# The up stage's results stored through POOL's DMA queue, and the third down operand loaded one stage earlier

## The chip, the cores and the metric

The kernel runs on one core of a Trainium2 chip. The metric is the device time of one execution in microseconds (us). Before the change three runs took 1323.78, 1328.26 and 1328.96 us, with a median of 1328.26 us.

## The reference

One transformer layer over 1024 latent tokens with 256 context tokens, in float32, with a model width of 1024. The part that matters here is its last one, the MLP, which is preceded by a modulated norm `h` of the mid-layer stream `x_mid`:

```python
def sq_relu_mlp(h, w1, w2):
    return jnp.square(jax.nn.relu(h @ w1)) @ w2

x = x_mid + gt_f * sq_relu_mlp(modulate(rms_norm(x_mid, g_ffn), sh_f, sc_f), w_ff1, w_ff2)
return rms_norm(x, g_final)
```

`w_ff1` is 1024 x 4096 and `w_ff2` is 4096 x 1024, so the activations between them are 1024 x 4096.

## The kernel before

**Arithmetic.** Every float32 operand of a product is split into a high and a low part (`split`, lines 102 to 104: a cast on ACT, line 103, then a subtraction on DVE, line 104). `mm3` (lines 96 to 100) then issues three matmuls: high by high (line 98), high by low (line 99), low by high (line 100).

**The up stage** (the first matrix of the MLP). Both MLP products are done with seven block products instead of eight (Strassen's scheme in Winograd's form). `w_ff1` is cut into 16 column groups p = 0 to 15 (`NP` is 16). For each p there are seven up products q = 1 to 7, and the list `order` (lines 1347 to 1352) says in which order the 112 pairs (p, q) are traced. The last eight are (15,2), (15,1), (14,3), (15,5), (15,6), (15,7), (15,4), (15,3). For each pair, `mm_1` issues 12 matmuls, and `post1` moves the result out of PSUM and combines it with the others. q = 6 and q = 7 add into the PSUM bank of q = 1, so the copies of lines 1177 and 1179 on ACT must have read the bank before the next of these products writes into it.

**The stores.** From one p come seven stores to DRAM: "a" after (p,1), 256 KB, and after (p,3) the blocks y, z and w, each as a high and a low part of 512 KB. `store_u` (lines 1146 to 1156) writes them. The high part is a cast on ACT into a new tile (line 1152), the low part a subtraction on DVE in place, and all seven DMAs are issued by SP (lines 1148, 1154, 1155). When they have landed, the tiles are free again.

**Tiles.** Nearly all large data lives in 45 equal tiles in SBUF (`Slots`, lines 35 to 50). A tile is taken from the front of a list of free ones when the code asks for it, and put at its end when the code is done with it. An instruction that writes into a reused tile waits until everything that used it before has finished, a store included. In the code's order the list holds 1 to 4 free tiles after the eight products from (0,7) to (3,6), behind which the first stores of y, z and w come, and 4 to 9 in the later regular part.

**The down stage** (the second matrix) goes through four blocks b of 1024 rows of `w_ff2`, with seven products each, `steps2 = (b, q)` with q in the order 2, 1, 6, 5, 3, 7, 4. One step is 48 matmuls. A step needs one operand from the stored activations (`load_u`: y, a, z, z, w, w, y) and one from `w_ff2` (B21, B11, B12 and B22 as loaded by `load_w2`, or their differences T1 to T3, made on DVE at line 1085 by `chain_w2`). `prep2` splits them. `load_u` issues the "a" blocks on SP's queue and y, z, w on POOL's (line 1237). `load_w2` issues on SP's (line 1211), as `load_w1` does for `w_ff1` (line 1092). The trace calls both weights `in_w_ff_dram`.

**The seam between the stages.** The loop over `order` already begins the down stage:

```python
        if s == len(order) - 11:
            load_w2(0, ("B21",))
            load_u(*steps2[0])
        if s == len(order) - 6:
            prep2(*steps2[0])
            load_w2(0, ("B11",))
            load_u(*steps2[1])
        if s == len(order) - 4:
            load_w2(0, ("B12", "B22"))
        if s == len(order) - 3:
            chain_w2(0)
        if s == len(order) - 2:
            prep2(*steps2[1])
```

The third step's operand, `steps2[2]` = (0,6), a z block, is loaded at the beginning of the first down step, and from then on each step s loads the operand of step s + 2 and prepares that of step s + 1. The tiles that `load_w2` gets for B12 and B22 of block 0 are those of z (low), w (high), w (low) and the working tile of p = 14. The tiles that `load_u` gets for the fourth step's operand (0,5) are those of y and z of p = 15, and `prep2` of (0,6) splits T2 into tiles of w of p = 15.

**Order on the engines.** The code's order is a priority. A planner sorts the instructions of every engine and queue by estimated times, so that an engine may hold a later line ahead of an earlier one. Each engine then works through its list in order and stops at the first instruction that has to wait.

Of the kernel before, what the change touches and what calls it, by code (L numbers as in the profile page):

```python
# [53 lines left out]
def hymba_block(ctx: ExitStack, tc: tile.TileContext, A, K, out):  # L54
    nc = tc.nc
    V, S, T, G = nc.vector, nc.scalar, nc.tensor, nc.gpsimd
# [7 lines left out]
    sl = Slots(slotp, NSLOT)  # L64
# [25 lines left out]
    def f(ap):  # L90
        return ap.bitcast(F32)

    def tt(o, a, b, op):
        V.tensor_tensor(out=o, in0=a, in1=b, op=op)  # L94
# [7 lines left out]
    def split(raw, hi, lo, eng=None):  # L102
        S.copy(out=hi, in_=raw)  # L103
        (eng or V).tensor_tensor(out=lo, in0=raw, in1=f(hi), op=ALU.subtract)  # L104
# [77 lines left out]
    order = "PDDPDDPPPPPPPPPP"  # L182
# [3 lines left out]
    for i, who in enumerate(order):  # L186
        q = (wa_pe if who == "P" else wa_dve)
        g, kt = q[sum(w == who for w in order[:i])]
        wa[g, kt] = load_wa(g, kt)
        if 3 <= i < 9:  # L190
            o, n, ap = rowsrc[i - 3]
# [194 lines left out]
    for t in range(NA):  # L386
# [8 lines left out]
        if t < NT:  # L395
            if t % 2 == 0:
                h = sl.get((2, 512))
# [139 lines left out]
    for i, t in enumerate(list(range(NT, NT + NC)) + list(range(NT))):  # L537
        if t % 2 == 0:
            h = sl.get((2, 512))
# [460 lines left out]
    for h in range(MH):  # L1000
        p = h // 2
# [40 lines left out]
    while pend:  # L1042
# [4 lines left out]
    NP, GB = FF // 256, 4  # L1047
    NB = NP // GB
    xm = [dramp.tile([P, 1024], F32, name=f"xm{t}") for t in range(NT)]
    ud = {(q, b, v): dramp.tile([P, n, GB, 512], F32, name=f"ud{q}{b}{v}")  # L1050
          for b in range(NB) for q, n in (("a", 1), ("y", 2), ("z", 2), ("w", 2))
          for v in ((0,) if q == "a" else (0, 1))}
# [30 lines left out]
    def pairop(eng, o, a, b, op):  # L1083
        for v in range(len(o)):
            eng.tensor_tensor(out=o[v][0], in0=a[v][0], in1=b[v][0], op=op)  # L1085
# [45 lines left out]
    def mm_1(p, q):  # L1131
        ps = bank(p, q)
        a = a1.pop((p, q))
        bh, bl = h2c[BOF[q]]
        for k in range(4):
            mm3(ps, a[0][:, 0, k], a[0][:, 1, k], bh[k // 2][0][:, k % 2, :], bl[k // 2][0][:, k % 2, :],
                q in (1, 2, 4, 5) and k == 0, k == 3, q in (3, 6, 7))
        sl.put(a)
        if p == NP - 1:
            sl.put(*bh, *bl)  # L1140
# [3 lines left out]
        S.activation(out=ap, in_=ap, func=AF.Square)  # L1144

    def store_u(q, p, r, ap):
        if q == "a":
            nc.sync.dma_start(out=ud[q, p // GB, 0][:, :, p % GB, :], in_=ap)
            return
        h = sl.get((2, 512), F32R)  # L1150
        lo = ap.bitcast(F32R)
        S.copy(out=h[0], in_=ap)  # L1152
        tt(lo, ap, f(h[0]), ALU.subtract)
        nc.sync.dma_start(out=ud[q, p // GB, 0][:, :, p % GB, :], in_=f(h[0]))
        nc.sync.dma_start(out=ud[q, p // GB, 1][:, :, p % GB, :], in_=f(lo))
        sl.put(h, r)

    def post1(p, q):
        ps = bank(p, q)
        if q == 2:  # L1160
            cq[p] = [sl.get((2, 512))]
            S.copy(out=cq[p][0][0][:, 0], in_=ps)
            unbank(p, q)
            return
        if q == 7:
            cq[p].append(sl.get((2, 512)))
        x_ = cq[p][0]
        c11, c12 = x_[0][:, 0], x_[0][:, 1]
        if len(cq[p]) > 1:
            y_ = cq[p][1]  # L1170
            c21, c22 = y_[0][:, 0], y_[0][:, 1]
        if q == 1:
            tt(c11, ps, c11, ALU.add)
            sqrelu(c11)
            store_u("a", p, x_, x_[0][:, 0:1])
        elif q == 6:
            S.copy(out=c12, in_=ps)
        elif q == 7:
            S.copy(out=c21, in_=ps)
            unbank(p, q)  # L1180
            tt(c22, bank(p, 5), c21, ALU.add)
        elif q == 4:
            tt(c21, c21, ps, ALU.subtract)
            unbank(p, q)
            sqrelu(c21)
            sqrelu(c22)
        elif q == 3:
            tt(c12, ps, c12, ALU.add)
            unbank(p, q)
            sqrelu(c12)  # L1190
            z, w = sl.get((2, 512)), sl.get((2, 512))
            s1, s2, s3, s4 = z[0][:, 0], z[0][:, 1], w[0][:, 0], w[0][:, 1]
            tt(s1, c12, c22, ALU.add)
            tt(s2, s1, c11, ALU.subtract)
            tt(s3, c11, c12, ALU.subtract)
            tt(s4, c21, s2, ALU.subtract)
            store_u("y", p, y_, y_[0])
            store_u("z", p, z, z[0])
            store_u("w", p, w, w[0])
            sl.put(x_)  # L1200
            cq.pop(p)
# [21 lines left out]
    def chain2_w2(b):  # L1223
        pairop(V, w2r[b, "B21"], w2r[b, "B21"], w2r[b, "T2"], ALU.subtract)
        w2r[b, "T4"] = w2r.pop((b, "B21"))
        sl.put(*w2r.pop((b, "T2")))
# [4 lines left out]
    def load_u(b, q):  # L1231
        n, k = UOF[q]
        vs = (0,) if n == "a" else (0, 1)
        ur[b, q] = [[sl.get((2, 512), F32 if n == "a" else F32R) for _ in range(GB // 2)] for _ in vs]
        for x_ in vs:
            for v, r in enumerate(ur[b, q][x_]):
                (nc.sync if n == "a" else nc.gpsimd).dma_start(out=r[0], in_=ud[n, b, x_][:, k, 2 * v:2 * v + 2, :])  # L1237

    def prep2(b, q):
        u_, w_ = ur.pop((b, q)), w2r[b, BOF[q]]  # L1240
        new = lambda: [[sl.get((2, 512), F32R) for _ in range(GB // 2)] for _ in range(2)]
        if len(u_) == 1:
            raw, u_ = u_[0], new()
            for v in range(GB // 2):
                split(raw[v][0], u_[0][v][0], u_[1][v][0])
            sl.put(*raw)
        ab[b, q] = [u_, new()]
        for v in range(GB // 2):
            split(w_[v][0], ab[b, q][1][0][v][0], ab[b, q][1][1][v][0])
        if q not in (2, 6):  # L1250
            sl.put(*w2r.pop((b, BOF[q])))
        if q == 6:
            chain2_w2(b)
# [93 lines left out]
    order = [(p, q) for q in (2, 1) for p in range(4)]  # L1347
# [11 lines left out]
    def w1_ahead(s):  # L1359
        for p, q in order[s:s + LEAD + 5]:  # L1360
            if p not in loaded:
                load_w1(p)
                loaded.add(p)
        for p, q in order[s:s + LEAD + 1]:
            if (p, q) not in prepped:
                prep1(p, q)
                prepped.add((p, q))

    steps2 = [(b, q) for b in range(NB) for q in (2, 1, 6, 5, 3, 7, 4)]
    for s, (p, q) in enumerate(order):  # L1370
        w1_ahead(s)
        mm_1(p, q)
        post1(p, q)
        print("S", s - len(order), s, p, q, len(sl.free), file=open("/tmp/sl.txt", "a"))
        if s == 0:
            pairop(V, b11, b12, b11, ALU.subtract)
            bsplit("T1", b11)
        if s == 4:
            pairop(V, b12, b22, b12, ALU.subtract)
            pairop(V, b11, b22, b11, ALU.subtract)  # L1380
            bsplit("T2", b11)
        if s == 6:
            pairop(V, b21, b11, b21, ALU.subtract)
            sl.put(*b11)
            bsplit("T3", b12, True)
        if s == 9:
            bsplit("T4", b21, True)
        if s == 13:
            bsplit("B22", b22, True)
# [10 lines that stand above are left out]
            chain_w2(0)  # L1400
        if s == len(order) - 2:
            prep2(*steps2[1])

    pF = Ring(list(range(8)))
    acc = {}
# [31 lines left out]

    for s, (b, q) in enumerate(steps2):
        last = b == NB - 1
        if s + 2 < len(steps2):  # L1440
            load_u(*steps2[s + 2])
        if s + 1 < len(steps2):
            if s > 0:
                prep2(*steps2[s + 1])
            if steps2[s + 1][1] == 2:
                chain_w2(b + 1)
        if b == NB - 2 and q == 2:
            load_bc5()
        if q == 5 and b + 1 < NB:
            load_w2(b + 1)  # L1450
        if last and q == 6:
            gfin = sl.get((1024,))
            nc.sync.dma_start(out=gfin[0], in_=A["g_final"].partition_broadcast(P))
        for k in range(4):
            mm_2(b, q, k)
            for fn in side.get((s, k), ()):
                fn()
            if last and q == 3:
                squares(k, 0)
                squares(k, 1)  # L1460
                final(k)
            if last and q == 7:
                squares(4 + k, 1)
            if last and q == 4:
                squares(4 + k, 0)
                final(4 + k)
        for x_ in ab.pop((b, q)):
            for h_ in x_:
                sl.put(*h_)
# [40 lines left out]
```

## Time and profile before

| | |
|---|---|
| Median of three runs | 1328.26 us (1323.78 to 1328.96) |
| The profiled execution | 1329.17 us |
| Its span, from the first to the last instruction | 1327.4 us, 18159 instructions |
| PE busy | 1275.3 us, 96% of the span |
| DVE, ACT, POOL busy | 73%, 49%, 6% |
| Up products, from about | 680 us to 1002 us |
| Moved by DMA | 216.73 MB, 163 GB/s on average |

The profile is of one execution, and all times of day in the text are microseconds from the beginning of its span. PE executes the matmuls, DVE and ACT the elementwise work, and SP and POOL issue DMAs (POOL does little else). A share of busy time is an average over all stages. The places where PE stands still are few and short, so they are read one by one in the order of time.

### The profile page before, as it was taken

What the parts mean: (1) busy time and instruction counts of PE and PEld (TensorE: products, weight loads), DVE (VectorE), ACT (ScalarE), POOL (GpSimd) and SP (SyncE); (2) the same over time, 40 slices, a digit from 0 to 9 for tenths busy, and PEclk for the clock granted to TensorE, in tenths of its full rate; (3) what the DMA queues carried; (4) which work ended last, traced back from release to release, by engine and by line L of the source; (5) the groups of instructions that cost most, each with busy time, mean ns of one, the idle gap of its engine ahead of it and who ended that gap; (6) DMA issues with size and microseconds to landing.
All of it is one profiled execution on the core that took longest, in us unless ns stands there. A gap on an engine that the chain in (4) does not pass through costs nothing.

```text
span 1327.4 us, 18159 instructions
## 1 busy us (share of the span) xinstructions
PE 1275.3 (96%) x6665; PEld 1086.9 (82%) x6665; DVE 973.9 (73%) x1950; ACT 644.5 (49%) x1349; POOL 73.4 (6%) x133
## 2 busy tenths in 40 slices
PE   7899999999999999999999799999987999999997
PEld 7788888999999898878788578887866788887885
DVE  5898576664777767984796788878767374876976
ACT  1851256754556545732475576766654231221233
POOL 0100000000000000000000000000001111111110
PEclk9999999999999999999999899999989999999999
DMA  9508401300001004362521577765799958577753
GB/s 348 213 3 290 153 28 53 100 13 0 1 9 36 9 25 143 104 214 96 162 84 51 211 276 247 270 225 205 245 338 341 373 159 289 202 257 259 215 158 125
DMA packets 98667, 216.73 MB, mean 163 GB/s; under 512 B 9353, under 2 KB 29522, under 8 KB 98578
## 3 DMA queue, kind: packets, MB, share of 16 engines
q1 hardware_dynamic: 81634, 156.56, 34.0%
q0 software_dynamic: 16368, 58.49, 13.3%
q8 instruction: 52, 0.85, 0.3%
q10 hardware_dynamic: 576, 0.53, 0.1%
q14 instruction: 37, 0.30, 0.1%
HBM read 148.70 MB, written 66.85 MB: 162 GB/s over the span
## 4 chain that ended last, share of the span: by engine, by line
PE 51%; issue 30%; DMA 8%; DVE 6%; ACT 4%; POOL 1%; SPq 0%; DVEq 0%; ACTq 0%; POOLq 0%
PE ps L100 15%; PE ps L98 15%; PE ps L99 15%; DMA u<-in_w_ff_dram 3%; DVE u L94 2%; PE ps L280 2%; DMA udw<-u 1%; DVE u L104 1%; ACT u L1152 1%; PE ps L238 1%; DMA udy<-u 1%; DMA u<-udy 1%; ACT u L103 1%; DVE u L502 1%; DMA u<-k_tri_dram 1%
## 5 line engine op out<-in xcount | busy, mean ns | idle before, releaser
L98 PE MATMUL ps<-u,u 128*128 128x512 f32 (+3 forms) x1664 | 621.5, 375 | 27.8 <-ACT u L103 8.0
L100 PE MATMUL ps<-u,u 128*128 128x512 f32 (+3 forms) x1664 | 613.3, 370 | 2.6 <-DVE u L94 1.7
L99 PE MATMUL ps<-u,u 128*128 128x512 f32 (+3 forms) x1664 | 614.8, 370 | 0.0
L98 PEld LDWEIGHTS ps<-u,u 128*128 128x128 f32 x1664 | 315.4, 190 | 86.0 <-ACT u L103 10.4
L100 PEld LDWEIGHTS ps<-u,u 128*128 128x128 f32 x1664 | 314.7, 189 | 54.8 <-DVE u L104 2.3
L99 PEld LDWEIGHTS ps<-u,u 128*128 128x128 f32 x1664 | 315.3, 189 | 49.0 <-issue 0.5
L103 ACT CAST u<-u 128x1024 fp32r<-128x1024 f32 (+3 forms) x199 | 168.1, 862 | 228.5 <-PE ps L99 66.5
L94 DVE TENSOR_TENSOR u<-ps,u 128x512 f32<-128x512 f32 (+3 forms) x318 | 201.7, 648 | 87.0 <-PE ps L100 62.0
L104 DVE TENSOR_TENSOR u<-u,u 128x1024 fp32r<-128x1024 f32 (+4 forms) x197 | 189.2, 982 | 59.6 <-ACT u L103 50.1
L94 DVE TENSOR_TENSOR u<-u,u 128x512 f32<-128x512 f32 (+2 forms) x128 | 114.9, 919 | 35.2 <-DMA u<-in_w_ff_dram 15.1
L863 DVE TENSOR_REDUCE mx<-ps 128x1 f32<-128x512 f32 (+1 forms) x96 | 55.0, 594 | 25.8 <-PE ps L862 25.7
L1152 ACT CAST u<-u 128x1024 fp32r<-128x1024 f32 x48 | 49.3, 1049 | 35.6 <-DVE u L94 29.8
L897 ACT CAST u<-ps 128x512 fp32r<-128x512 f32 (+1 forms) x96 | 45.1, 530 | 21.2 <-PE ps L895 21.2
L1085 DVE TENSOR_TENSOR u<-u,u 128x1024 f32<-128x1024 f32 x40 | 47.7, 1216 | 3.4 <-DMA u<-in_w_ff_dram 3.3
L1143 ACT ACTIVATE u<-u 128x512 f32<-128x512 f32 x64 | 40.1, 627 | 20.2 <-DVE u L94 19.9
L874 ACT ACTIVATE u<-ps,nm 128x512 f32<-128x512 f32 x64 | 43.6, 691 | 11.8 <-DVE nm L867 11.8
L1144 ACT ACTIVATE u<-u 128x512 f32<-128x512 f32 x64 | 40.3, 631 | 1.1
L427 DVE SCALAR_TENSOR_TENSOR u<-u,sc,u 128x1024 f32<-128x1024 f32 x28 | 35.8, 1279 | 4.5 <-DMA u<-in_w_ada_dram 4.2
L1237 POOL DMA_DIRECT2D u<-udy x32 | 16.9, 534 | 371.7 <-DVE u L104 314.9
L858 PE MATMUL ps<-u,u 128*128 128x512 f32 (+1 forms) x96 | 37.1, 387 | 0.4 <-ACT u L837 0.2
L280 PE MATMUL ps<-u,u 128*128 128x128 f32 x224 | 29.1, 295 | 8.6 <-DMA u<-in_w_ada_dram 8.6
L104 DVE TENSOR_TENSOR u<-tmp,u 128x512 fp32r<-128x512 f32 x32 | 21.8, 687 | 19.3 <-ACT u L103 19.3
(209 smaller groups left out, 1290.1 us busy)
## 6 DMA issues: line engine op xcount, KB each, us to landing
u<-in_w_ff_dram SPq DMA_DIRECT2D x64, 512.0 KB, 7.0
u<-in_w_ada_dram SPq DMA_DIRECT2D x48, 512.0 KB, 5.5
udy<-u SPq DMA_DIRECT2D x32, 512.0 KB, 3.6
udz<-u SPq DMA_DIRECT2D x32, 512.0 KB, 3.8
udw<-u SPq DMA_DIRECT2D x32, 512.0 KB, 5.3
u<-udy POOLq DMA_DIRECT2D x32, 512.0 KB, 7.0
u<-udz POOLq DMA_DIRECT2D x32, 512.0 KB, 6.6
u<-udw POOLq DMA_DIRECT2D x32, 512.0 KB, 7.7
```

What stands on the lines that cost most here:

```text
L94: V.tensor_tensor(out=o, in0=a, in1=b, op=op)
L98: T.matmul(ps, lhsT=lh, rhs=rh, start=start, stop=False, **kw)
L99: T.matmul(ps, lhsT=lh, rhs=rl, start=False, stop=False, **kw)
L100: T.matmul(ps, lhsT=ll, rhs=rh, start=False, stop=stop, **kw)
L103: S.copy(out=hi, in_=raw)
L104: (eng or V).tensor_tensor(out=lo, in0=raw, in1=f(hi), op=ALU.subtract)
L280: T.matmul(mps[g][j // 4][:, j % 4, :], lhsT=w[:, j * P:(j + 1) * P], rhs=rhs, start=first and j % 4 == 0, stop=last and j % 4 == 3)
L863: V.reduce_max(out=mx[:, kb:kb + 1], in_=ps[:, 0:n], axis=AX.X)
L874: S.activation(out=dst[kb], in_=ps[:, 0:n], func=AF.Exp, scale=SCALE, bias=nm, accum_out=su[:, kb:kb + 1])
L897: S.copy(out=hi, in_=ps[:, 0:m, :])
L1085: eng.tensor_tensor(out=o[v][0], in0=a[v][0], in1=b[v][0], op=op)
L1152: S.copy(out=h[0], in_=ap)
```

## The change

The seven stores of each p from 0 to 14 are issued by POOL instead of SP. Those of p = 15 stay on SP. The operand of the third down step, (0,6), is loaded after `prep2` of the second, in front of the last up product, instead of at the beginning of the first down step. A line that printed to a file while the program was traced is gone; it put nothing into the program.

```diff
     def store_u(q, p, r, ap):
+        dq = nc.sync if p == NP - 1 else nc.gpsimd
         if q == "a":
-            nc.sync.dma_start(out=ud[q, p // GB, 0][:, :, p % GB, :], in_=ap)
+            dq.dma_start(out=ud[q, p // GB, 0][:, :, p % GB, :], in_=ap)
             return
         h = sl.get((2, 512), F32R)
         lo = ap.bitcast(F32R)
         S.copy(out=h[0], in_=ap)
         tt(lo, ap, f(h[0]), ALU.subtract)
-        nc.sync.dma_start(out=ud[q, p // GB, 0][:, :, p % GB, :], in_=f(h[0]))
-        nc.sync.dma_start(out=ud[q, p // GB, 1][:, :, p % GB, :], in_=f(lo))
+        dq.dma_start(out=ud[q, p // GB, 0][:, :, p % GB, :], in_=f(h[0]))
+        dq.dma_start(out=ud[q, p // GB, 1][:, :, p % GB, :], in_=f(lo))
         sl.put(h, r)
...
         if s == len(order) - 2:
             prep2(*steps2[1])
+            load_u(*steps2[2])
...
     for s, (b, q) in enumerate(steps2):
         last = b == NB - 1
-        if s + 2 < len(steps2):
+        if 0 < s < len(steps2) - 2:
             load_u(*steps2[s + 2])
```

## Rows read from the trace of the kernel before

**Rows 1.** The page's busy time: engine, busy us, share, instructions.

```profile
PE 1275.3 (96%) x6665; PEld 1086.9 (82%) x6665; DVE 973.9 (73%) x1950; ACT 644.5 (49%) x1349; POOL 73.4 (6%) x133
```

**Rows 2.** Windows: stretch, length, busy us (instructions) by engine, PE clock, DMA share, GB/s.

```profile
850.00:900.00 50.00, 50.00 (x222) 41.31 (x221) 39.42 (x56) 33.94 (x55) 0.00 (x0) 1.00 0.75 261
...
980.00:990.00 10.00, 6.07 (x27) 4.69 (x25) 6.24 (x7) 4.18 (x6) 0.00 (x0) 0.92 0.97 356
...
1010.00:1020.00 10.00, 10.00 (x46) 8.29 (x45) 7.42 (x7) 3.40 (x4) 1.59 (x3) 1.00 1.08 394
```

**Rows 3.** Timeline of PE: start, us, instruction, [idle before <-what ended it].

```profile
741.02 0.50 PE L98 MATMUL ps<-u,u 128*128 128x512 f32 x1 [3.38 <-ACT u L103]
...
750.36 0.80 PE L98 MATMUL ps<-u,u 128*128 128x512 f32 x1 [3.76 <-ACT u L103]
...
908.14 0.50 PE L98 MATMUL ps<-u,u 128*128 128x512 f32 x1 [1.07 <-ACT u L1177]
...
991.82 0.80 PE L98 MATMUL ps<-u,u 128*128 128x512 f32 x1 [5.75 <-ACT u L1177]
...
995.56 0.39 PE L98 MATMUL ps<-u,u 128*128 128x512 f32 x1
...
1028.60 2.90 PE L98 MATMUL ps<-u,u 128*128 128x512 f32 x6 [7.48 <-DMA u<-udz]
...
1032.90 0.39 PE L100 MATMUL ps<-u,u 128*128 128x512 f32 x1
...
1035.33 0.97 PE L98 MATMUL ps<-u,u 128*128 128x512 f32 x3 [0.89 <-ACT u L103]
```

**Rows 4.** Timeline of ACT ahead of the longer halt at 986 us.

```profile
988.34 1.04 ACT L103 CAST u<-u 128x1024 fp32r<-128x1024 f32 x1 [3.28 <-DMA u<-in_w_ff_dram]
989.29 1.99 ACT L1152 CAST u<-u 128x1024 fp32r<-128x1024 f32 x2
991.19 0.58 ACT L1177 COPY u<-ps 128x512 f32<-128x512 f32 x1
```

**Rows 5.** The chain that ended last, in order of time: start, us, what.

```profile
733.47 5.40 DMA udy<-u
...
744.83 4.78 DMA udz<-u
...
892.40 8.18 DMA u<-in_w_ff_dram
...
978.19 10.08 DMA u<-in_w_ff_dram
...
993.88 6.16 DMA udw<-u
1000.05 13.66 DMA u<-in_w_ff_dram
1013.81 4.63 DVE u L1085 x4
...
1020.18 3.42 DVE u L94 x3
```

**Rows 6.** Timeline of POOL at the seam.

```profile
1000.56 1.06 POOL L1237 DMA_DIRECT2D u<-udz  x2 [22.31 <-PE ps L100]
...
1021.82 0.53 POOL L1237 DMA_DIRECT2D u<-udz  x1 [9.92 <-DVE u L94]
```

**Rows 7.** Issues from 760 to 950 us: queue, count, size, median us to landing.

```profile
udz<-u SPq DMA_DIRECT2D x22, 512.0 KB, 3.7
...
u<-in_w_ff_dram SPq DMA_DIRECT2D x19, 512.0 KB, 6.3
```

**Rows 8.** Tile xm, 600 to 700 us: POOL's eight stores of 512 KB.

```profile
DMA to landing us min/median/max: 2.9/3.8/6.6
```

**Rows 9.** Tile udz, 985 to 1005 us: the transfers of z.

```profile
L1237 POOL DMA_DIRECT2D u<-udz x4: 527/532/537, 1000.6 to 1002.7; - x4
...
DMA to landing us min/median/max: 7.0/8.9/10.9
```

## What was predicted

> **What bounds the kernel now.** The page comes first: TensorE is busy for 96% of the span and POOL for 6% [rows 1]. Such a kernel can only win where PE stands still or runs at the low clock, so the next view is the windows. From 850 to 900 us, in the regular part of the up stage, PE is busy for all 50.00 us, 222 matmuls at the full clock, 0.226 us each [rows 2]. There the change can't give anything, whatever it does to DMA. It can only matter at the two ends of the up stage, and PE's timeline has the places [rows 3]. Two halts of 3.38 and 3.76 us lie at 741 and 750 us, one of 1.07 us at 908 us, one of 5.75 us ahead of 991.82 us, one of 7.48 us ahead of 1028.60 us and 0.89 us soon after. After each of the two long ones the clock is at its lower level for a while: from 991.82 to 995.56 us nine matmuls take 3.74 us instead of 9 x 0.226 = 2.03 us, 1.7 us lost, and from 1028.60 to 1032.90 us ten take 4.30 instead of 2.26 us, 2.0 us lost [rows 3]. So the seam costs 5.75 + 1.7 = 7.45 us at its first halt (I call it C) and 7.48 + 2.0 + 0.89 = 10.4 us at its second (D); the early halts A and B cost 7.1 us.
>
> Who holds them up? C names a copy on ACT, line 1177. On ACT that copy stands behind two casts of results (line 1152) and a cast at 988.34 us that waited for a weight [rows 4]: the first tile of B11, issued by SP at 978.19 us and landed 10.08 us later [rows 5]. The chain of waits leads on from there: the last store of p = 14 is issued at 993.88 and lands after 6.16 us, its tile takes a load of `w_ff2` at 1000.05, which needs 13.66 us, and only then DVE goes on with T2 (line 1085) at 1013.81. Behind that in DVE's list stand the low parts of y, z and w of p = 15, at 1020.18 us [rows 5]. When the low part of y is done, its tile can take a load of z, and POOL issues it at 1021.82 us after a wait for DVE [rows 6]. PE names a load of z at 1028.60, 6.8 us later [rows 3].
>
> So which z is it? The third operand's four loads are issued from 1000.56 us on, when the last up product has freed their tiles [rows 6], and the z transfers of that window land within 7.0 to 10.9 us [rows 9], by about 1014, well ahead of the end of the second down step at 1021.1 us (1028.60 - 7.48). The z that PE waits for is therefore the fourth step's, issued at 1021.82, which the planner's order multiplies first. The third operand is not late in this trace.
>
> **The change part by part.** *Third operand earlier.* Four issues of 0.53 us on POOL [rows 6] move from about 1001 us to about 987 us (in the code's order they now get tiles that the products (15,6) and (15,7) free, and those lie around C). It removes no wait of its own. Its 2.1 MB now go while DMA moves 356 GB/s and is 97% busy [rows 2], 5.9 us of transfer in front of, or beside, the last stores of p = 14. Bounds: nothing, if the planner puts those stores first, to 5.9 us on the chain above, if all of it lies ahead. I take the middle, 2.9 us.
>
> *Stores on POOL.* 105 of 112 stores move. On SP, the weights now have in front of them no store and none of the waits for ACT and DVE that the stores bring. Between 760 and 950 us, with five stores of 512 KB ahead of each pair, a weight takes 6.3 us to land [rows 7]. The one of C took 10.08 us. I expect 6.3 us in its place: stores and loads of y are still in flight on the other queue. ACT's cast then starts 3.8 us sooner, and so do the two casts and the copy behind it; C shrinks from 5.75 to 2.0 us, and a halt of that size leaves the clock alone as that of 1.07 us does, so 5.5 us are won. Bounds: 0 (the weight lands as late as now) and 7.45 us (C gone).
>
> Then the chain of D. The last store of p = 14 follows ACT 3.8 us sooner, at 990.1; it needs its 6.16 us and the 2.9 us from above, and its tile is free at 999.2. The weight that goes there takes 6.3 instead of 13.66 us, since on its queue only weights and the "a" load are left, and lands at 1005.5 instead of 1013.7, 8.2 us sooner. What follows up to PE's restart (DVE's chain, the low parts, the load of z) took 14.9 us (1013.7 to 1028.60) and I keep it, since p = 15 still stores on SP and DVE's list is the same. PE restarts at 1020.4. The second step ends at 1021.1 - 5.5 = 1015.6, so D is still 4.8 us long and keeps its slow clock and the 0.89 us behind it. The gain up to PE's restart, C's included, is 8.2 us. Bounds: 0, and 7.45 + 10.4 = 17.9 us, if all weights land in time.
>
> *The early halts.* A and B hang on the landing of a store into whose tile ACT wants to write: y after 5.40 and z after 4.78 us [rows 5], each with a `w_ff1` load ahead of it on SP's queue. POOL's own stores of this size land after 2.9 to 6.6 us, 3.8 in the median [rows 8], and SP's of z after 3.7 [rows 7], so the queue itself is no slower. At the median, A and B would lose 1.6 and 1.0 us; at 6.6 us they would gain 1.2 and 1.8. I take half of the gain, 1.3 us.
>
> *The halt at 908 us* hangs on a weight that took 8.18 us [rows 5] behind stores: 1.1 us won.
>
> *Issuing.* POOL does nothing else in the regular part (0.00 us busy [rows 2]), and 105 issues of 0.53 us are 56 us spread over 300 us, seven to each p, whose seven products take 7 x 12 x 0.226 = 19 us. What could stand behind a waiting store on POOL are the loads of y for the first down step, due some 30 us later. This costs nothing as long as those loads are early; ahead of C they would have to slip by more than that.
>
> *Sum:* 8.2 + 1.3 + 1.1 = 10.6 us from the profiled execution's own 1329.17 us gives 1318.6. That execution lies 0.9 us above the median of the runs, 1328.26, so I predict 1318 us. Half a percent, 6.6 us, is about what a measurement of this kernel can tell from no change, so "faster" begins at 1321.6 and "slower" at 1334.9.
>
> One rule speaks against this. In the window of C the 16 DMA engines are 97% busy [rows 2]: what gives a weight its earlier landing must come from something else in flight, not from a second queue as such. The Trainium skill, "DMA: Bandwidth & Descriptors", section "Issuing engines are not separate DMA queues", says that DMAs of any engine run on the same 16 DMA engines and that spreading them saves only the time of the sequencer. By that alone C and D stay as they are, and the sum is the 0 of the bounds above, 1328 us. The trace has not yet a stretch that decides it.
>
> **The rivals.** *1. The weights land no sooner.* DMA at 356 GB/s ahead of the seam and 394 GB/s at 1010 us [rows 2] is near the most that any row here shows, and the third operand adds 2.1 MB there sooner. If loads and stores merely share, the weight of C keeps its 10 us, and with up to 5.9 us for the third operand D grows by as much as C might lose. Time: 1322 to 1334, the middle 1328. For it: those two rows. Against it: a weight now waits for its own queue's bytes first, and ahead of it these fall from five stores to none.
>
> *2. The seam closes.* If the weight of C lands within 4.5 us, C goes, and if w low of p = 14 goes out ahead of the third operand, its tile is free by 994 and the weight there by 1000; PE restarts at 1015 against a second step ending at 1013.7. C and D are worth 17.9 us, less 1; with the 1.1 us of 908 and 2.6 of A and B that is 20.6 us, and the time 1308. Against it: both have to go right at once, and p = 15's low parts stay behind T2 on DVE.
>
> *3. Slower: stores through POOL land late where tiles are short.* Around 725 to 790 us only 1 to 4 tiles are free and ACT's next cast waits for a store. The mechanism is one: the landing through POOL. If it grows to 8.3 us and more, 4.5 over the median of rows 8, A and B grow by 4.5 us each, and the next two groups of stores (p = 2 and 3), which today just pass, halt PE for about 4.5 us with 1.7 us of slow clock: 21 us, less the 10.6 won, 1338 us. It decides from about 17 us, that is, from a landing some 3.5 us later than the median of rows 8 (4 x 3.5 + 2 x 1.7 = 17.4). Against it: the longest of those eight is 6.6 us, and the issues on POOL at the seam stay at 0.53 us while DVE is three quarters busy [rows 2, 6]. The Trainium skill, "SBUF — State Buffer", section "SBUF: two separate sides", warns of just this: a DMA from GpSimd has its descriptors written by that engine, and these can starve while VectorE is in a two-port mode. POOL's rows here show no such starving, and the subtractions that fill DVE in this stage are two-input ones, which the page does not count among those modes.
>
> **How the numbers follow.** The forecast, both halts at the seam shrunk: 0.46, with a range of its own from 1311 to 1322. Rival 2, 1300 to 1311: 0.16. Rival 1, 1322 to 1334: 0.25. Rival 3 and a planner's order with new halts of the size of C, above 1334: 0.13. Faster takes the first two, 0.62; same 0.25; slower 0.13. With a tenth or so left out at the upper end and a few hundredths at the lower, the range is 1304 to 1334.
>
> **What would show it.** Right: stores of udy, udz, udw on POOL's queue, the weights of the regular part landing in 4 to 5 instead of 6.3 us, PE's halt behind the copy of line 1177 at 2 us or less without a slow clock, T2 on DVE at about 1005 us. The halt at the second step's end should still name a load of z or a cast into a tile of p = 15. Wrong: the cast of B11 still waiting 3 us for its weight (rival 1), or ACT waiting between 730 and 790 us for udy or udz for more than 5 us at a time (rival 3). What makes the prediction wrong soonest is the planner: other estimated times can put another instruction ahead on ACT, DVE or PE, and one halt of C's kind is worth 7 us.

## The result and the profile after

The changed kernel takes 1363.03 us (median, 1360.25 to 1365.65), the kernel before 1328.61 us (1323.78 to 1333.52) beside it: a ratio of 1.0259, interval 1.0215 to 1.0302, so 34 us slower. The prediction said 1318 us and gave "slower" 0.13. It was wrong in sign. The profiled execution has a span of 1360.2 us, 32.8 us more than before.

The page's busy time of the changed kernel, to be read beside [rows 1]:

```profile
PE 1295.3 (95%) x6665; PEld 1095.5 (81%) x6665; DVE 972.4 (71%) x1950; ACT 645.6 (47%) x1349; POOL 143.4 (11%) x238
```

PE, DVE and ACT run as many instructions as before, and POOL issues 105 DMAs more. PE's extra 20 us of busy time are the same matmuls taken more slowly. Windows of the changed kernel, with the columns of [rows 2]; the first is the stretch of the regular part that the prediction called full, the next four are short pieces of the following groups, then comes the seam, and last the whole stretch in which the two kernels differ:

```profile
850.00:900.00 50.00, 44.36 (x189) 34.30 (x188) 32.52 (x47) 31.02 (x50) 10.54 (x16) 1.00 0.58 205
...
900.00:903.00 3.00, 3.00 (x9) 2.35 (x8) 3.00 (x6) 0.98 (x2) 0.00 (x0) 0.50 0.00 0
...
924.00:927.00 3.00, 3.00 (x8) 2.32 (x8) 3.00 (x6) 1.04 (x2) 0.00 (x0) 0.50 0.00 0
...
945.00:948.00 3.00, 2.45 (x11) 1.76 (x10) 3.00 (x6) 1.98 (x4) 0.00 (x0) 1.00 0.23 87
948.00:951.00 3.00, 3.00 (x15) 2.34 (x14) 2.96 (x6) 2.01 (x3) 0.00 (x0) 1.00 0.03 5
...
1010.00:1020.00 10.00, 6.29 (x28) 4.88 (x26) 5.29 (x7) 3.76 (x5) 0.73 (x2) 0.97 1.07 390
...
690.00:1090.00 400.00, 360.36 (x1460) 283.66 (x1459) 273.04 (x367) 228.11 (x352) 83.33 (x130) 0.94 0.65 227
```

The same stretch in the kernel before:

```profile
690.00:1090.00 400.00, 375.54 (x1608) 305.61 (x1607) 299.54 (x394) 235.93 (x362) 19.04 (x36) 0.97 0.70 244
```

The loss is in the regular part first: 189 matmuls in 50 us where 222 fitted before. The timeline of PE in the changed kernel, against [rows 3], shows why:

```profile
743.58 0.79 PE L98 MATMUL ps<-u,u 128*128 128x512 f32 x1 [2.85 <-ACT u L103]
...
752.48 0.50 PE L98 MATMUL ps<-u,u 128*128 128x512 f32 x1 [2.85 <-ACT u L103]
...
876.03 0.50 PE L98 MATMUL ps<-u,u 128*128 128x512 f32 x1 [1.71 <-ACT u L103]
...
897.86 0.50 PE L98 MATMUL ps<-u,u 128*128 128x512 f32 x1 [1.61 <-ACT u L103]
899.14 0.50 PE L100 MATMUL ps<-u,u 128*128 128x512 f32 x1 [0.55 <-DVE u L104]
...
921.92 0.50 PE L98 MATMUL ps<-u,u 128*128 128x512 f32 x1 [2.30 <-ACT u L103]
...
966.21 0.50 PE L98 MATMUL ps<-u,u 128*128 128x512 f32 x1 [1.30 <-ACT u L103]
...
1021.93 0.80 PE L98 MATMUL ps<-u,u 128*128 128x512 f32 x1 [5.63 <-ACT u L1178]
...
1058.09 0.79 PE L98 MATMUL ps<-u,u 128*128 128x512 f32 x1 [5.07 <-ACT u L103]
...
1068.33 1.65 PE L98 MATMUL ps<-u,u 128*128 128x512 f32 x3 [4.19 <-ACT u L103]
```

The early halts are a little shorter. But from 860 us on every column group has a halt at a cast (0.89 to 2.30 us) and one of 0.55 us behind it, and after those of 1.61 and 2.30 us the clock is at its lower level (0.50 in the windows from 900 and from 924 us, nine and eight matmuls in 3 us where 15 fit at 948). Added up from 690 to 1090 us, PE's halts come to 39.4 us after and 24.3 before, 15.1 us more. The granted clock in that stretch is 0.94 after and 0.97 before; what is missing to 1, times 400 us, is 24 and 12 us, so 12 us more (an estimate, for PE does not work all of that time). Together that is about 27 of the 32.8 us. The rest is not parted; the page's 20 us of slower matmuls are more than the clock's 12.

What happens in one group is seen by following one z tile. The timeline of SP, POOL and DVE in the changed kernel, from a store of low z to the next:

```profile
885.36 0.67 POOL L1156 DMA_DIRECT2D udz<-u  x1 [0.46 <-DVE u L94]
...
890.22 0.37 SPq L1092 DMA_DIRECT2D u<-in_w_ff_dram  x1
...
895.86 0.69 DVE L94 TENSOR_TENSOR tmp<-u,u 128x512 f32<-128x512 f32 x1 [2.22 <-DMA u<-in_w_ff_dram]
896.47 0.68 DVE L94 TENSOR_TENSOR tmp<-tmp,u 128x512 f32<-128x512 f32 x1
897.19 0.69 DVE L94 TENSOR_TENSOR u<-u,tmp 128x512 f32<-128x512 f32 x1
897.80 0.68 DVE L94 TENSOR_TENSOR u<-u 128x512 f32<-128x512 f32 x1
898.40 0.68 DVE L104 TENSOR_TENSOR u<-tmp,u 128x512 fp32r<-128x512 f32 x1
...
907.61 0.67 POOL L1156 DMA_DIRECT2D udz<-u  x1 [0.46 <-DVE u L94]
```

The store lands, its tile takes the next group's second weight (890.22), that lands after 5.5 us, and DVE, which has stood still for it, goes on: a ring of 22.25 us, while PE needs 19 us for a group. The same stretch of DVE in the kernel before, and SP's next store of low z:

```profile
897.51 0.68 DVE L94 TENSOR_TENSOR u<-u,tmp 128x512 f32<-128x512 f32 x1
898.11 0.69 DVE L104 TENSOR_TENSOR u<-tmp,u 128x512 fp32r<-128x512 f32 x1
898.72 0.68 DVE L94 TENSOR_TENSOR u<-u 128x512 f32<-128x512 f32 x1
900.67 0.69 DVE L94 TENSOR_TENSOR tmp<-u,u 128x512 f32<-128x512 f32 x1 [1.27 <-DMA u<-in_w_ff_dram]
...
908.72 0.51 SPq L1155 DMA_DIRECT2D udz<-u  x1
```

The instruction that waits for the weight is the sum of the next group's weights (line 94 into `tmp`). Before, it stands behind the rest of the current product 6, which fills the time. After, it stands in front. From it to the next store of low z it is 11.75 us after (895.86 to 907.61) and 8.05 before (900.67 to 908.72). That is another order on DVE, not another transfer. As the two programs list it (`u_9072` and `u_9073` are the group's weights, `u_9229` and `u_9230` the next one's, `u_9256` the low part of product 6; the numbers are places in the list, and the changed program has the sum in front like this in the groups p = 9 to 14):

```
before: 1399 tmp<-tmp,u_9072 | 1401 u_9073<-u_9073,tmp | 1402 u_9256<-tmp,u_9256 | 1404 tmp<-u_9229,u_9230
after:  1400 tmp<-u_9229,u_9230 | 1401 tmp<-tmp,u_9072 | 1402 u_9073<-u_9073,tmp | 1404 u_9256<-tmp,u_9256
```

So two suspects came out of the trace: the order, and the transfers (w lands after 6.7 us instead of 4.9 in the median, and SP now waits for the tile of z).

### The profile page after: what moved, and what is told of

Its sections match the earlier page's. It is cut to its first block, busy times and chain, and to the rows that moved or that the text cites. A ratio compares the mean times of both kernels' runs of the same rounds, so it can differ in the third digit from the quotient of the medians.

```text
span 1360.2 us, 18197 instructions
## 1 busy us (share of the span) xinstructions
PE 1295.3 (95%) x6665; PEld 1095.5 (81%) x6665; DVE 972.4 (71%) x1950; ACT 645.6 (47%) x1349; POOL 143.4 (11%) x238
## 4 chain that ended last, share of the span: by engine, by line
issue 47%; PE 34%; DMA 6%; DVE 5%; POOL 4%; ACT 2%; POOLq 0%; DVEq 0%; ACTq 0%; SPq 0%
PE ps L100 10%; PE ps L98 10%; PE ps L99 10%; DMA udw<-u 2%; DVE u L94 2%; PE ps L280 2%; DMA u<-in_w_ff_dram 1%; DMA udy<-u 1%; DVE u L104 1%; DVE u L502 1%; POOL udw L1156 1%; DVE u L1085 1%; PE ps L238 1%; DMA u<-k_tri_dram 1%; POOL udy L1156 1%
## 5 line engine op out<-in xcount | busy, mean ns | idle before, releaser
L98 PEld LDWEIGHTS ps<-u,u 128*128 128x128 f32 x1664 | 318.3, 191 | 100.6 <-ACT u L103 33.6
L100 PEld LDWEIGHTS ps<-u,u 128*128 128x128 f32 x1664 | 317.7, 191 | 63.9 <-DVE u L104 9.5
L99 PEld LDWEIGHTS ps<-u,u 128*128 128x128 f32 x1664 | 318.3, 191 | 50.8 <-DVE u L104 1.0
L933 POOL DMA_DIRECT2D y_dram<-tmp x7 | 5.3, 754 | 319.3 <-ACT tmp L931 319.3
L280 PEld LDWEIGHTS ps<-u,u 128*128 128x128 f32 x224 | 29.7, 218 | 9.3 <-issue 5.0
```

The costliest lines, as they stand in the source:

```text
L98: T.matmul(ps, lhsT=lh, rhs=rh, start=start, stop=False, **kw)
L99: T.matmul(ps, lhsT=lh, rhs=rl, start=False, stop=False, **kw)
L100: T.matmul(ps, lhsT=ll, rhs=rh, start=False, stop=stop, **kw)
L280: T.matmul(mps[g][j // 4][:, j % 4, :], lhsT=w[:, j * P:(j + 1) * P], rhs=rhs, start=first and j % 4 == 0, stop=last and j % 4 == 3)
```

## The experiments

All times are medians; each ratio is to the kernel before on the same chip.

| kernel | us | ratio | interval |
|---|---|---|---|
| e1: stores on POOL alone | 1356.91 | 1.0217 | 1.0169 to 1.0266 |
| e2: third operand alone | 1330.57 | 1.0010 | 0.9997 to 1.0024 |
| e3: changed, next casts pinned | 1354.19 | 1.0173 | 1.0143 to 1.0202 |
| e4: before, sum ahead | 1338.22 | 1.0061 | 1.0038 to 1.0083 |
| e7: weights on POOL, stores on SP | 1348.81 | 1.0135 | 1.0106 to 1.0164 |
| e8: stores and weights on POOL | 1331.84 | 1.0000 | 0.9985 to 1.0016 |
| e9: changed, group order put back | 1347.94 | 1.0123 | 1.0089 to 1.0157 |
| e10: before, with e9's pins | 1332.13 | 1.0007 | 0.9987 to 1.0028 |
| e11: only w on POOL | 1362.88 | 1.0222 | 1.0198 to 1.0247 |
| e12: a, y, z on POOL | 1358.77 | 1.0206 | 1.0181 to 1.0232 |
| e13: stores of p = 13, 14 on POOL | 1332.51 | 1.0001 | 0.9983 to 1.0019 |
| e14: e1 in the order of before | 1342.86 | 1.0075 | 1.0043 to 1.0106 |
| e15: before in the order of e1 | 1360.91 | 1.0227 | 1.0190 to 1.0263 |
| e16: e8 in the order of before | 1337.40 | 1.0052 | 1.0034 to 1.0070 |
| e17: e7 in the order of before | 1342.56 | 1.0096 | 1.0069 to 1.0122 |

**Which part of the change.** e1 takes the third operand's part back, e2 leaves the stores on SP:

```diff
-            load_u(*steps2[2])
...
-        if 0 < s < len(steps2) - 2:
+        if s + 2 < len(steps2):
```
```diff
-        dq = nc.sync if p == NP - 1 else nc.gpsimd
+        dq = nc.sync
```

> Only the stores on POOL, the third operand as before. Theory (the planner's order): the stores' move makes the planner put the next column group's first use of its weights ahead of the current group's sixth product on DVE and ACT, so all of the loss in the regular part stays: 1357 to 1367 us. Rival 1 (stores through POOL land later and tiles come free later): the same, 1357 to 1367. Rival 2 (the third operand's early load is what costs): 1324 to 1334.

> Only the third operand earlier, the stores on SP as before. Theory and rival 1: 1322 to 1334 us, the regular part from 850 to 900 us without a halt. Rival 2: 1355 to 1365.

The stores carry nearly all of the loss, and the third operand costs nothing that can be told.

**The one swap that the trace shows.** e3 queues the casts and low parts of the next group's products 1, 2 and 5 behind product 6 of the current group (`done6` holds that cast and low part). e4 does the reverse to the kernel before: the next sum is traced ahead of product 6's subtraction.

```diff
+        if q in (1, 2, 5) and p - 1 in done6:
+            with ExitStack() as st:
+                for i in done6[p - 1]:
+                    st.enter_context(tc.issue_after(i))
+                prep1_(p, q)
+            return
```
```diff
+            ahead = V.tensor_tensor(out=ws[p + 1], in0=wquad(p + 1, 1, 0), in1=wquad(p + 1, 1, 1), op=ALU.add)
+            with tc.issue_after(ahead.ins):
+                tt(ws[p], ws[p], wquad(p, 0, 0), ALU.subtract)
```

> The changed kernel, with the next group's preparation (products 1, 2 and 5) queued on ACT and DVE behind the current group's sixth, as it was before the change; stores still on POOL. Theory: the halts of 1 to 2 us for every group go, 1322 to 1342 us, and PE from 900 to 950 us is busy for 49 us or more at the full clock. Rival 1: the stores land no sooner, 1355 to 1367, with halts in that stretch as now.

> The kernel before, stores on SP, third operand as before, but with the sum of the next group's two weight tiles put on DVE ahead of the current group's subtraction for product 6, as the changed kernel's planner did. Theory: halts of 1 to 3 us for most groups, 1345 to 1368 us. Rival 1: stores still land through SP, so 1324 to 1334.

The swap is real but small. e4 loses 0.6%, between the ranges of its theory and of its rival. e3 misses its theory's range: by the ratios it recovers 0.9 points of 2.6, but beside e1, which ran with it, the intervals overlap. "This one swap is the whole cause" fell.

**POOL, or the separation.** e7 exchanges the queues and e8 puts both in POOL's; e9 puts the sum back too, and e10 is its control.

```diff
-            nc.sync.dma_start(out=w1r[p][kq][0], in_=w_ff1[kq * 512:(kq + 1) * 512, p * 256:(p + 1) * 256].rearrange("(k p) c -> p k c", p=P))
+            (nc.gpsimd if p >= 4 else nc.sync).dma_start(out=w1r[p][kq][0], in_=w_ff1[kq * 512:(kq + 1) * 512, p * 256:(p + 1) * 256].rearrange("(k p) c -> p k c", p=P))
...
-                nc.sync.dma_start(out=r[0], in_=w2v[i, :, g:g + 2, j * 512:(j + 1) * 512])
+                (nc.sync if b else nc.gpsimd).dma_start(out=r[0], in_=w2v[i, :, g:g + 2, j * 512:(j + 1) * 512])
```
```diff
+                with tc.issue_after(low.ins):
+                    done6[p].append(V.tensor_tensor(out=ws[p + 1], in0=wquad(p + 1, 1, 0), in1=wquad(p + 1, 1, 1), op=ALU.add).ins)
```

> The kernel before with all stores on SP, and the loads of weights (w_ff1 from column group 4 on, and the first block of w_ff2) issued by POOL instead: the same separation of stores and loads, with the engines exchanged. Theory A (the separation is the cause: the planner reckons a weight early as soon as no store stands ahead of it in its queue, puts the weight's consumers first on DVE and ACT, and the engines then wait for it): about as slow as with the stores on POOL, 1350 to 1362 us, with PE halts of 1 to 2.5 us in each column group. Theory B (stores issued by POOL leave later and land later, so tiles come free later): the stores are on SP, so 1325 to 1335 us and no halts in the groups from p = 5 to 13.

> Stores of p = 0 to 14 on POOL, third operand as before, and the loads of weights (w_ff1 from column group 4 on, first block of w_ff2) on POOL as well, so that stores and loads stand in one queue as in the kernel before, only on another engine. Theory A (separation): the order of the engines is nearly that of before and weights stay behind the stores, so 1326 to 1338 us. Theory B (stores through POOL): 1348 to 1365 us, since each store still costs POOL 0.67 us and w lands after 6.7 us.

> The changed kernel with the order of before put back for column groups 5 to 15: on DVE the subtraction and low part of product 6, then the sum of the next group's weights, then the low parts of the next group's products 1, 2 and 5; the casts on ACT likewise. The pins of the third experiment had left that sum behind the low parts, where DVE's stretch from the weight's landing to the store of low z was 9.5 us instead of 8.1. Theory A in its form 'order alone': the groups' period returns from 20.8 to about 19.1 us and the time to 1330 to 1340 us. Theory B, or any loss from the transfers themselves: above 1348 us, with halts in the groups still there.

> Control: the kernel before with the same pins as the kernel of the run before this one. All theories: 1326 to 1333 us, as before, because the order that the pins ask for is the one it has already.

This tells most. With every store and weight on POOL nothing is lost, although POOL issues all of them (w lands after 5.8 us). With no store of the up stage on POOL but the weights there, 1.35% is lost. So the loss is not the price of issuing from POOL. In e7 the sum again stands ahead of product 6's low part, in e8 behind it, as before: the list follows the separation, whichever engine issues. e9 recovers half, misses the range of "order alone" and keeps halts of 0.6 to 3.1 us in nearly every group, now behind the copy of product 6; e10 shows that its pins by themselves cost nothing.

**Part of the stores.** The condition for `dq` becomes `q == "w"` in e11, `q != "w"` in e12, and `p in (13, 14)` in e13, the prediction's term for the seam by itself.

```diff
-        dq = nc.sync if p == NP - 1 else nc.gpsimd
+        dq = nc.gpsimd if q == "w" and p < NP - 1 else nc.sync
```

> Only the two stores of w of p = 0 to 14 on POOL, those of a, y and z on SP as before, third operand as before. DVE's sum of the next weights stands behind product 6 as before, so the swapped order is absent. Theory A2 (besides the order, the loss comes from weights that are no longer held back behind the stores of w in one queue, and travel beside them, so that w lands after 6 us or more instead of 4.9 and ACT's casts wait for its tile): 1336 to 1348 us, stores of w landing after 6 to 7 us. Theory C (the order is the whole of it): 1327 to 1334 us.

> The complement: a, y and z of p = 0 to 14 on POOL, 75 of the 105 stores that the change moves, and w on SP in front of the weights as before; third operand as before. The sum on DVE again stands behind product 6. Theory A2: weights stay behind the stores of w, which land after 5.5 us or less, so 1325 to 1336 us. Theory C: the same. A loss through POOL's stores as such (theory B): three quarters of it or so, 1346 us and more.

> Only the stores of p = 13 and 14 on POOL, third operand as before: the prediction's term for the seam by itself, with the regular part of before. As predicted (the weights at the seam land in 6.3 us with no store ahead of them in their queue): 1318 to 1324 us, the halt at the copy near 986 us 2 us instead of 5.75. Rival (weights and stores share the transfer engines and land no sooner): 1326 to 1336 us, the halt 4 us or more.

Both lose it all, with the sum where it was. e11 missed every range, and e12 came out where theory B had it. But B is a loss for each store on POOL, and moving 30 stores costs as much as moving 75 or 105, while e8, with all of them on POOL, loses nothing: the loss isn't a sum over stores. The timeline of ACT in e11 shows one more swap:

```profile
914.84 0.62 ACT L103 CAST u<-tmp 128x512 fp32r<-128x512 f32 x1 [4.25 <-DMA udw<-u]
915.37 0.58 ACT L1180 COPY u<-ps 128x512 f32<-128x512 f32 x1
```

A cast into a tile of w now stands ahead of the copy of product 7 (line 1179 before), and everything on ACT behind it waits 4.25 us for the store. From 760 to 960 us such waits for udw add up to 44.5 us in e11, 38.1 in e12 and 2.2 before (line, what it waited for, us in total, times, longest):

```profile
ACT u L103 <- DMA udw<-u: 44.5, 14, 4.9
...
ACT u L103 <- DMA udw<-u: 38.1, 16, 4.2
...
ACT u L103 <- DMA udw<-u: 2.2, 1, 2.2
```

No run moves this swap by itself, so that it makes the loss of e11 and e12 is argued. In e13 the regular part is that of before, and the seam gains nothing. PE's timeline there, and the chain that ended last:

```profile
989.54 0.80 PE L98 MATMUL ps<-u,u 128*128 128x512 f32 x1 [2.87 <-ACT u L1178]
...
1025.54 0.79 PE L98 MATMUL ps<-u,u 128*128 128x512 f32 x1 [4.63 <-ACT u L103]
...
1036.66 1.22 PE L98 MATMUL ps<-u,u 128*128 128x512 f32 x2 [5.24 <-ACT u L103]
```
```profile
976.05 9.94 DMA u<-in_w_ff_dram
...
991.01 9.86 DMA udw<-u
1000.89 10.71 DMA u<-in_w_ff_dram
```

The halt at C is halved, as the prediction wanted, but not by a faster landing: the weight still takes 9.94 us and was issued 2.1 us sooner. The store of w follows 2.9 us sooner and takes 3.7 us longer, the pair of store and weight takes 20.6 us instead of 19.8 [rows 5], and PE stands still at D for 9.9 us (4.63 + 5.24) instead of 8.4 (7.48 + 0.89).

**Order against transfers.** The trace can't part the two, so e14 and e15 hold one and move the other. Every instruction of DVE, ACT and PE from the first up product on is queued in exactly the order of another kernel (`ORDER` is that list; `done` are the instructions as traced):

```diff
+    def queue(self, tc, runs):
+        seq = [self.done[a + i] for a, n in runs for i in range(n)]
+        for one, two in zip(seq, seq[1:]):
+            tc.add_manual_dep(two, one.name, mybir.DependencyInfo(mybir.DependencyClass.NoSync, mybir.DependencyReason.DATA),
+                              reason="order")
...
+    for e, k in ((V, "V"), (S, "S"), (T, "T")):
+        e.queue(tc, ORDER[k])
```

> Stores of p = 0 to 14 on POOL as in the changed kernel, third operand as before, and from the first up product to the end every instruction of DVE, ACT and PE queued in exactly the order of the kernel before. Theory order (POOL's queue makes the planner reckon weights and free tiles earlier, it reorders DVE and ACT, and engines that work their list in turn then wait for what lands later than reckoned): 1326 to 1337 us, no halt of over 1 us in each group of the regular part. Theory transfers (the weights travel beside the stores, tiles come free later, whatever the order): 1345 to 1360 us, ACT waiting for udw 10 us and more between 760 and 960 us as in the changed kernel.

> The reverse: all stores on SP as before, and DVE, ACT and PE queued in exactly the order of the kernel with the stores on POOL (the first experiment). Theory order: 1345 to 1360 us, halts of 1 to 2.5 us in each group at a cast. Theory transfers: 1328 to 1338 us.

Two things could spoil such a pair. The pins could cost something themselves: they do not, for the kernel before, pinned in its own order, comes out as the same program, instruction for instruction, and so does e1. And the lists of SP and POOL are not held: in e15 SP's differs from that of before in 21 of 333 places, mostly stores of one group exchanged, but in none of the groups p = 7 to 12, in which the halts below lie; in e14 POOL's differs from that of e1 in 15 of 242.

e15 has the stores of before, but for these exchanges, and the list of e1, and loses what e1 loses: 1.0227 against 1.0217, just past the 1345 to 1360 us of the theory of order. Its timeline of ACT, DVE and PE (all lines are that of the noting helper):

```profile
911.13 0.62 ACT L159 CAST u<-u 128x512 fp32r<-128x512 f32 x1 [3.35 <-DMA u<-in_w_ff_dram]
911.15 0.69 DVE L159 TENSOR_TENSOR tmp<-u,u 128x512 f32<-128x512 f32 x1 [4.02 <-DMA u<-in_w_ff_dram]
...
913.15 0.73 PE L159 MATMUL ps<-u,u 128*128 128x512 f32 x2 [1.97 <-ACT u L159]
...
914.43 0.96 PE L159 MATMUL ps<-u,u 128*128 128x512 f32 x3 [0.55 <-DVE u L159]
```

This is the changed kernel's signature, the 0.55 us included, with SP issuing every store and w landing after 4.7 us. e14 is the other way about: stores on POOL, the list of before. Two thirds of the loss are gone (0.75% against 2.17%), but e14 lies between the ranges of its two theories. The waits of its ACT from 760 to 960 us hold what the transfers still do:

```profile
ACT u L157 <- DMA udw<-u: 10.6, 13, 4.7
ACT u L157 <- DMA u<-in_w_ff_dram: 1.0, 2, 0.8
```

The waits for weights are as good as gone (10.4 us on ACT in the changed kernel), those for w's tile stay (10.6 us, before 2.2).

**The rest.** Is the 0.75% of e14 POOL's, or that of two queues? The edits are e8's and e7's with e14's order.

> Stores of p = 0 to 14 and the loads of weights (w_ff1 from column group 4 on, first block of w_ff2) both on POOL, and DVE, ACT and PE queued in exactly the order of before. With the order held, the kernel with stores on POOL and weights on SP was 0.75% slower. Theory one queue (what is left of the loss is that a weight no longer stands behind the stores of w): 1327 to 1336 us, no different from before. Theory POOL (what is left comes from POOL's issues of 0.67 us or its transfers): 1340 us and more.

> Stores on SP, the same loads of weights on POOL, and DVE, ACT and PE queued in exactly the order of before. Theory one queue: the same 0.75% as with the stores on POOL, 1338 to 1347 us, since the weights again travel beside the stores. Theory POOL's stores: 1327 to 1336 us, since no store is on POOL.

Neither theory holds alone. Two queues without a store on POOL cost 0.96% (e17, in the range of "one queue"), but one queue on POOL costs 0.52% in this order (e16, between the two ranges) and nothing in its own (e8). What is seen is that the order of before costs 0.5 to 1% with each of the three other arrangements of the transfers. Which transfer does it stays open.

## Why the prediction was wrong

**The step that failed** is the first: "There the change can't give anything, whatever it does to DMA", and with it the assumption that the engines' lists stay as they are ("DVE's list is the same", said of the seam). From a PE that is busy for all 50 us the text concluded that the regular part was indifferent. It could not win, but it could lose: the ring through the store of z, its tile, the next weight and DVE had hardly any slack over PE's own 19 us (DVE already waited 1.27 us for the weight at 900.67, and PE halted for 1.07 us in that group [rows 3]), and the order that fitted it came out of the planning and was not given. The text named the planner as what "makes the prediction wrong soonest", but priced it as one halt of C's kind. It was a halt in every group from 860 us on, 0.89 to 2.30 us at the cast and 0.55 us behind it, and only 189 matmuls from 850 to 900 us where 222 fitted.

**What was shown and what is argued.** Shown: the order alone brings a loss as large as that of e1 (e15); putting the old order back takes away two thirds (e14), so that order and transfers do not simply add up; separating stores from weights changes the order, whichever engine issues which (e7, e8). Argued only: why the planner does so, presumably because it reckons a weight, or the tile of a store, as early once less stands ahead of it in its queue. In the trace the wait moved from the queue to the tile: SP's loads of `w_ff1` waited for stores of z 192.6 us from 760 to 960 us, and 2.2 us before:

```profile
SPq L1092 <- DMA udz<-u: 192.6, 18, 26.4
...
SPq L1092 <- DMA udz<-u: 2.2, 2, 1.1
```

That wait is not the price itself: e14, with a third of the loss, has 182.4 us of it.

**The terms of the sum.**
- *Weights land in 4 to 5 us.* 5.4 in the median from 760 to 950 us, 6.3 before [rows 7]: right in direction, worth nothing.
- *C shrinks to 2.0 us.* 5.63 us in the changed kernel, behind the same copy. ACT waits 4.24 and 3.01 us for weights there. Rival 1 was right here.
- *D's chain 8.2 us sooner.* Store of w 9.63 us and weight 10.24 us, 19.9 together, against 6.16 and 13.66, 19.8 together [rows 5]. What one transfer wins the other loses. The Trainium skill, "DMA: Bandwidth & Descriptors", section "Issuing engines are not separate DMA queues", says that spreading DMAs over issuing engines saves only sequencer time. At this seam (390 GB/s and a DMA share of 1.07 in the changed kernel, 395 and 1.06 in e13 from 980 to 990 us) e13 agrees with its 1.0001. By that sentence the seam's term would have been 0 instead of 8.2 us.
- *Early halts, 1.3 us.* 2.85 + 2.85 + 0.20 us after, 3.38 + 3.76 + 0.69 before: 1.9 us won. Right in size, but by luck: the term was simply half of what a median landing would win, and e13, with these stores on SP, already has 2.67 + 3.23 + 0.57 us.
- *The halt at 908 us, 1.1 us.* That halt is gone (by the count of matmuls the same one starts at 929.29 in the changed kernel, without a wait), but its group has 2.30 and 0.55 us at a cast in its place.
- *Third operand, 2.9 us out of 0 to 5.9.* e2: 0.1%, with an interval of -0.4 to 3.2 us. It is at the lower bound.
- *Issuing.* A store took POOL 0.67 us instead of 0.53, and POOL's busy time grew by 70.0 us for 105 issues. By e8 that costs nothing.
- *A halt of 2 us leaves the clock alone.* Not as a rule: the halts of 1.61 and 2.30 us were each followed by a stretch at the lower level, and so was that of 1.30 us at 966 us (0.52 from 968 to 971 us), while that of 1.71 us at 876 us was not (1.00 from 879 to 882 us). By the estimate above some 12 of the 33 us are clock.

**Rival 3** had the right sign for a wrong reason. Its mechanism, landings through POOL of 8.3 us, did not come: y lands after 3.7 us, z after 4.2, w after 6.7, and e8 sends all through POOL without loss.

## What to carry to other kernels

Where a planner orders the engines by estimated times, moving DMAs to another queue can also change the order on every engine, so compare the lists before pricing the transfers. A bound engine that is busy all the time says what cannot be won; whether it can be lost has to be read from the tightest ring through buffers, stores and loads behind it. To part order from transfers, hold the order of one version and move the transfers of the other, in both directions.

## What the runs showed of the hardware

- Issuing a store of y or z took POOL 0.67 to 0.68 us and SP 0.51 to 0.53 us.
- Halts of 0.89 and 0.55 us in one group left the granted clock at 1.00 (945 to 951 us), and so did 1.71 and 0.55 us (879 to 882 us). 1.30 and 0.55 us were followed by 3 us at 0.52 (from 968 us), 1.61 and 0.55 us by 3 us at 0.50 (from 900 us). The length of a halt alone did not decide.
- At the seam, a store and the load behind it took 19.8 to 20.6 us together in three kernels (before, after, e13), however the pair was divided.
